# Decay exponents from running sums by head, and the backward weighing on the vector engine

## The chip, the cores and the metric

The kernel runs on one core of a Trainium2 chip. The metric is the device time of one execution in microseconds (us), lower is better. The core has five engines that work side by side, each taking its own instructions in a fixed order: TensorE (PE, matrix products, with its weight loads shown as PEld), VectorE (DVE), ScalarE (ACT), GpSimd (POOL), and SyncE (SP), which here only issues transfers. They wait for each other through semaphores. SBUF is the memory they work in; PSUM holds the results of PE and is read by DVE and ACT.

## What is computed

One layer of an encoder over 256 tokens of 2048 channels, all float32. The part that matters is the bidirectional state-space mixer: with 16 heads, two groups and chunks of 128 tokens, it needs for each head, direction and chunk a 128 x 128 matrix of decays, the exponential of a difference of running sums.

```python
da = jnp.moveaxis((dt * a).reshape(b, c, q, g, e), 2, -1)
acum = jnp.cumsum(da, axis=-1)
...
seg = acum[..., :, None] - acum[..., None, :]
decay = jnp.exp(jnp.where(causal, seg, -jnp.inf))
cb = jnp.einsum("bclgn,bcsgn->bcgls", cmc, bmc)
y_diag = jnp.einsum("bcgls,bcgels,bcsgep->bclgep", cb, decay, xdt)
```

The backward direction does the same on the flipped sequence, and both are added. The state-space mixer stands beside a pooling mixer; both read one input projection (`w_in`) and go through one output projection (`w_out`). A gated convolutional feed-forward network and a gated embedding follow; the change doesn't touch them.

## The kernel before

Every large product is split: a float32 matrix is kept as a rounded high half and a remainder, and three products (high-high, high-low, low-high) replace one. `split` (L139) makes the halves of a weight block: ACT copies the high half (L150), DVE subtracts for the low one (L151). Blocks come through a ring of three raw buffers (`raw`, L154) by transfers on SP's queue, and the halves live in rings of five. `page` (L71) hands out 13 pages of 2048 columns in a ring, `mid` (L74) three of 1024. PSUM has eight banks: six for `main` accumulators, two for `misc`.

The order in time is this. The projection `dtu` (time steps and pooling input) runs first, until about 53 us. Then three slabs of `xbc` follow by `feature_major` (L317): slab 2, slab 0, slab 1, four blocks of weights each, 48 products of 256 columns a block. Behind each slab come `times_rows` (L402), the five-tap convolution `conv` (L410; four ACT instructions `cv` on L416, 16 DVE instructions on L422), a tanh on ACT (L622) and a last product on DVE (L624). Then the projection `z` runs by `token_major` (L285), and `w_out` (`wo`, its products named `woa`) from about 208 us.

Between the blocks the list `work` (L671 to L705) gives small jobs: each block, on ending, takes one entry (`aside`, L194). A scheduler that works on the whole program then decides where each instruction stands on its engine, so that the jobs mostly, not always, stand where the list has them. The jobs that matter:

- `seg_prep(i)` (L552): four POOL products of 512 columns (L558) make, for four heads of one chunk, the time steps `da` (as high half `dah` and remainder `dal`) masked by a triangle, for both directions. `seg(i)` (L562): four PE products with a triangle (`m_gt`, `m_lt`) turn them into the exponents of both directions in one PSUM buffer; ACT takes the exponential into `E` (L567). There are eight of each.
- `decays` (L540): four small PE products `dps` and an exponential give the decays to and from the chunk borders (`dec`).
- `pool_mix`, `pool_map` (L574, L583): the pooling mixer; `pool_map` empties its PSUM buffer by four pairs of ACT and DVE instructions (`cath`, L188, and `catl`, L189).
- `cb` (L596): the products of B and C, masked into `cbm`.
- `weigh(t, g)` (L627): weighs the decays of eight heads: POOL multiplies the backward part (L630), DVE adds the forward part in eight instructions (L635) and multiplies into `E` (L639).
- `xs_turn` (L609): PE transposes of a slab (`xt`), emptied by ACT into `xs` (L614). `far(t)` (L644): POOL makes `xd` from `xs` (L646). `skip(t)`: POOL, L650. `mix(t, g)` (L653): PE product `yo` of `xd`, then DVE, POOL, eight PE products `yd` of `E` and `xs`, and DVE.

`seg`, `decays`, `pool_mix`, `pool_map`, `cb`, `xs_turn` and `mix` all take their PSUM from the two `misc` buffers, in turn.

Of the kernel before, what the change touches and what calls it, by code (L numbers as in the profile page):

```python
# [21 lines left out]
H = 16  # L22
# [29 lines left out]
def build(nc, a, out):  # L52
# [5 lines left out]
    with tile.TileContext(nc) as tc, \  # L58
# [24 lines left out]
        def misc(name):  # L83
            return pc.tile([P, 512], F32, tag="misc", name=name)

        def mm(o, lhsT, rhs, start, stop):
            nc.tensor.matmul(o, lhsT, rhs, start=start, stop=stop, skip_group_check=True)  # L87


        ep = early.enter_context(tc.tile_pool(name="early", bufs=1))  # L90
# [18 lines left out]

        xt = [ep.tile([P, V_SCW + L], F32, name="xt0")] + [page(f"xt{i}") for i in (1, 2)]  # L110
        vt = cp.tile([P, V_N - V_SCW], F32, name="vt")
        small = ep.tile([P, 80 + 512], F32, name="small")

        last, sums_ = {}, {}

        def load(dst, src, ahead=False):

            with tc.issue_after(last["dma"]) if last and not ahead else nullcontext():
                return ins(nc.sync.dma_start(dst, src))
# [8 lines left out]

        last["dma"] = load(xt[0], a["x_cols"][:, :V_SCW + L])
        dtb, alog, dsk = small[:, :32], small[:, 32:64], small[:, 64:80]  # L130
        mask = small[:, 80:].rearrange("p (m f) -> p m f", m=4)

        def vec(i):
            return xt[0][:, i:i + 1] if i < V_SCW else vt[:, i - V_SCW:i - V_SCW + 1]
# [302 lines left out]
        for u in range(0, NK, 2):  # L437
            r = [wp.tile([P, 2048], F32, tag="raw", bufs=3, name=f"dtur{u}") if u else r0, page(f"dtur{u + 1}")]
# [37 lines left out]
        with tc.issue_after(half[0]), tc.issue_after(half[1]):  # L476
            xs_ = [page(f"x{t}") for t in range(2)]
            for t in range(2):
                load(xs_[t], x[t * P:(t + 1) * P, :])
            rx = row_rstd("rx", xs_)  # L480
            m_gt, m_lt = (ep.tile([P, P], F32R, name=n) for n in ("m_gt", "m_lt"))
            nc.vector.tensor_copy(m_gt, mask[:, 2, :])
            nc.vector.tensor_copy(m_lt, mask[:, 3, :])
            aneg = ep.tile([P, 32], F32, name="aneg")
            nc.scalar.activation(aneg, alog, AF.Exp)
            nc.gpsimd.tensor_scalar(aneg, aneg, -1.0, None, op0=ALU.mult)

# [17 lines left out]
        for t in range(2):  # L505
# [3 lines left out]
                                    op0=ALU.mult)  # L509
# [20 lines left out]
        dah = ep.tile([P, 2, 32], F32R, name="dah")  # L530
        dal = ep.tile([P, 2, 32], F32, name="dal")
        nc.vector.tensor_tensor(da, dt, aneg.unsqueeze(1).to_broadcast([P, 2, 32]), op=ALU.mult)
        nc.vector.tensor_copy(dah, da)
        nc.vector.tensor_sub(dal, da, dah.bitcast(F32))

# [14 lines left out]
        steps = {}  # L550

        def seg_prep(i):  # L552
            t, q = divmod(i, 4)
            ap_ = page(f"ap{i}", F32R).rearrange("p (a h l) -> p a h l", a=4, h=4)
            for j in range(4):
                d, src = j // 2, (dah.bitcast(F32), dal)[j % 2]
                hs = slice(d * H + 4 * q, d * H + 4 * q + 4)
                nc.gpsimd.tensor_tensor(ap_[:, j], src[:, t, hs].unsqueeze(2).to_broadcast([P, 4, P]),  # L558
                                        mask[:, d, :].unsqueeze(1).to_broadcast([P, 4, P]), op=ALU.mult)
            steps[i] = ap_  # L560

        def seg(i):  # L562
            t, q = divmod(i, 4)
            sps, ap_ = misc(f"seg{i}"), steps.pop(i)
            for j in range(4):
                mm(sps, (m_gt, m_lt)[j // 2], ap_[:, j].rearrange("p h l -> p (h l)"), j == 0, j == 3)
            nc.scalar.activation(ee[t][:, q * 512:(q + 1) * 512], sps, AF.Exp)  # L567


        cat = Panel.__new__(Panel)  # L570
# [56 lines left out]
        def weigh(t, g):  # L627

            w = mid(f"w{t}{g}")
            nc.gpsimd.tensor_tensor(w.rearrange("p (h l) -> p h l", h=8),  # L630
                                    cbm[:, 1, g, t, :].unsqueeze(1).to_broadcast([P, 8, P]),
                                    dt[:, t, H + 8 * g:H + 8 * g + 8].unsqueeze(2).to_broadcast([P, 8, P]),
                                    op=ALU.mult)
            for h in range(8):
                nc.vector.scalar_tensor_tensor(w[:, h * P:(h + 1) * P], cbm[:, 0, g, t, :],  # L635
                                               dt[:, t, 8 * g + h:8 * g + h + 1], w[:, h * P:(h + 1) * P],
                                               op0=ALU.mult, op1=ALU.add)
            es = ee[t][:, g * 1024:(g + 1) * 1024]
            nc.vector.tensor_mul(es, es, w)  # L639
# [28 lines left out]
        def job(f, *args):  # L668
            return lambda: f(*args)

        xd = {}  # L671
        work.extend([
            [job(seg_prep, 0)],
            [job(seg_prep, 1), job(pool_mix, 0), job(pool_mix, 1)],
            [job(seg_prep, 2), job(pool_mix, 2), job(pool_mix, 3), job(decays)],
            [job(seg_prep, 3), job(seg, 0)],
        ])
        bc = xbc(2)
        work.extend([
            [job(seg_prep, 4), job(seg, 1), job(pool_map, 0), job(pool_map, 1)],  # L680
            [job(seg_prep, 5), job(seg, 2), job(cb, bc, 0), job(cb, bc, 1)],
            [job(seg_prep, 6), job(seg, 3), job(pool_map, 2), job(pool_map, 3)],
            [job(seg_prep, 7), job(seg, 4), job(weigh, 0, 0)],
        ])
        xa = xbc(0)
        work.extend([
            [job(seg, 5), job(weigh, 0, 1)],
            [job(seg, 6), job(xs_turn, xa, 0)],
            [job(seg, 7), job(weigh, 1, 0)],
            [job(weigh, 1, 1)],  # L690
        ])
        xb = xbc(1)
        y = page("y")
# [1 line left out]

        work.extend([
            [],
            [],
            [],
            [job(xs_turn, xb, 1)],  # L700
            [job(far, 1), job(skip, 0), job(far, 0), job(skip, 1)],
            [job(mix, 0, 0)],
# [11 lines left out]
        for t in range(2):  # L714
# [13 lines left out]
            r = rms(f"yn{t}", [ss], rz[t][:, 1:2], n=2)  # L728
# [97 lines left out]
        h = [page(f"h{t}") for t in range(2)]  # L826
# [122 lines left out]
        for half in range(2):  # L949
# [13 lines left out]
            for t in range(2):  # L963
                for n, (o, c0) in enumerate(columns(acc[t])):
                    c1 = c0 + o.shape[-1]
                    c = slice(half * 1024 + c0, half * 1024 + c1)
# [4 lines left out]
                    if end:  # L971
# [3 lines left out]
                                                   op0=ALU.add, op1=ALU.mult)  # L975
                    q = tiny(f"gq{t}{half}{n}", 1)
# [11 lines left out]
def laid_out(a):  # L988

    def cols(*vs):  # L990
        return np.concatenate([v.reshape(-1, P).T for v in vs], axis=1)

    return {
        "x_cols": np.concatenate([cols(a["mix_norm_pre"][0]),
                                  a["x"][0].T.reshape(NK, P, L).transpose(1, 0, 2).reshape(P, NK * L)], axis=1),
        "p_t": a["p"][0, 0].T.reshape(2, P, L).transpose(1, 0, 2),
        "columns": np.concatenate([
            cols(a["ssd_conv_w"][0], a["ssd_conv_b"][0], a["ssd_norm"][0], a["pool_scale"][0], a["ffn_norm_pre"][0],
                 a["ffn_conv_w"][0], a["ple_norm_pre"][0], a["ffn_conv_b"][0]),
            np.broadcast_to(np.concatenate([a[n][0].reshape(-1) for n in ("ssd_dt_bias", "ssd_a_log", "ssd_d")]),  # L1000
                            (P, 80)),
            masks().transpose(1, 0, 2).reshape(P, 4 * P)], axis=1),
    }


def masks():
    j = np.arange(P)[:, None]
    l = np.arange(P)[None, :]
    return np.stack([j <= l, j >= l, j > l, j < l]).astype(np.float32)


def constants():
# [17 lines left out]
```

## Time and profile before

| | |
|---|---|
| time, median of 3 runs | 1143.8 us (1143.8 to 1144.74) |
| the profiled execution | 1143.09 us, its span 1141.3 us |
| mean granted clock of TensorE | 0.997 |
| chain that ended last | PE 90%, DVE 6%, ACT 1%, DMA 1%, issue 1%, POOL 1% |
| `xbc` slab 2, 0, 1 on PE, first product | 52.8 us, 82.2 us, 124.1 us |
| `z` on PE, first product | 151.5 us |
| `woa` on PE, first product | 207.8 us |

The span is the time between the first and the last recorded instruction; the device time has 1.8 us more around it. A busy time of an engine is the sum over its instructions, and matmuls overlap, so that two that start 0.47 us apart are shown with 0.62 us each. What the time follows is the chain that ended last: it is traced back from the last instruction, each time to what released it. The busy shares over the whole span hide the stretch from 80 to 170 us, where DVE is busy for 80 to 100% of each 10 us and POOL for up to 100%.

### The profile page before, as it was taken

What the parts mean: (1) busy time and instruction counts of PE and PEld (TensorE: products, weight loads), DVE (VectorE), ACT (ScalarE), POOL (GpSimd) and SP (SyncE); (2) the same over time, 40 slices, a digit from 0 to 9 for tenths busy, and PEclk for the clock granted to TensorE, in tenths of its full rate; (3) what the DMA queues carried; (4) which work ended last, traced back from release to release, by engine and by line L of the source; (5) the groups of instructions that cost most, each with busy time, mean ns of one, the idle gap of its engine ahead of it and who ended that gap; (6) DMA issues with size and microseconds to landing.
All of it is one profiled execution on the core that took longest, in us unless ns stands there. A gap on an engine that the chain in (4) does not pass through costs nothing.

```text
span 1141.3 us, 15449 instructions
## 1 busy us (share of the span) xinstructions
PE 1122.0 (98%) x6018; PEld 966.0 (85%) x6018; DVE 868.8 (76%) x1140; ACT 611.0 (54%) x830; POOL 124.9 (11%) x124
## 2 busy tenths in 40 slices
PE   9998999999999999999999999999999999999996
PEld 9997987888888888888888888888888888778885
DVE  6579896699876666666766756668888888789895
ACT  6633543565674554444544544545555565656562
POOL 0274504200110000000000000000000000001001
PEclk9999999999999999999999999999999999999999
DMA  9952347555556555555555565556566656666552
GB/s 358 341 184 75 111 151 267 200 160 190 172 190 205 196 190 185 184 185 186 189 191 193 181 204 186 185 184 222 157 212 221 200 170 220 194 221 205 181 196 74
DMA packets 129866, 220.09 MB, mean 193 GB/s; under 512 B 3713, under 2 KB 96769, under 8 KB 128897
## 3 DMA queue, kind: packets, MB, share of 16 engines
q1 hardware_dynamic: 129232, 217.70, 57.4%
q0 software_dynamic: 272, 1.05, 0.5%
q8 instruction: 47, 0.77, 0.3%
q10 hardware_dynamic: 288, 0.36, 0.1%
q14 instruction: 27, 0.21, 0.1%
HBM read 216.99 MB, written 2.10 MB: 192 GB/s over the span
## 4 chain that ended last, share of the span: by engine, by line
PE 90%; DVE 6%; ACT 1%; DMA 1%; issue 1%; POOL 1%; DVEq 0%; POOLq 0%; ACTq 0%
PE va L87 22%; PE ga L87 21%; PE dna L87 15%; PE gt L87 7%; PE woa L87 7%; PE dtu L87 4%; PE z L87 4%; PE xbc L87 3%; DVE cv L422 2%; PE dns L87 1%; PE ple L87 1%; DMA dn134r<-w_ffn_down 1%; PE dn0s L87 1%; DVE w L635 1%; DVE xb_0l L151 1%
## 5 line engine op out<-in xcount | busy, mean ns | idle before, releaser
L87 PE MATMUL ga<-wox,ug_0h 128*128 128x512 f32 x352 | 125.5, 395 | 0.0
L87 PE MATMUL ga<-wox,ug_1h 128*128 128x512 f32 x352 | 125.1, 394 | 0.0
L87 PE MATMUL va<-wox,uv_1h 128*128 128x512 f32 x352 | 124.8, 393 | 0.0
L87 PE MATMUL va<-wox,uv_0h 128*128 128x512 f32 x352 | 124.8, 393 | 0.0
L87 PE MATMUL ga<-wox,ug_1l 128*128 128x256 f32 x352 | 99.1, 282 | 0.0
L87 PE MATMUL ga<-wox,ug_0l 128*128 128x256 f32 x352 | 99.1, 282 | 0.0
L87 PE MATMUL va<-wox,uv_1l 128*128 128x256 f32 x352 | 99.1, 281 | 0.0
L87 PE MATMUL va<-wox,uv_0l 128*128 128x256 f32 x352 | 99.1, 281 | 0.0
L87 PEld LDWEIGHTS va<-wox,uv_0h 128*128 128x128 f32 x352 | 66.1, 188 | 15.0
L87 PEld LDWEIGHTS va<-wox,uv_1h 128*128 128x128 f32 x352 | 66.1, 188 | 15.0
L87 PEld LDWEIGHTS ga<-wox,ug_0h 128*128 128x128 f32 x352 | 66.1, 188 | 14.9
L87 PEld LDWEIGHTS ga<-wox,ug_1h 128*128 128x128 f32 x352 | 66.1, 188 | 14.9
L87 PE MATMUL dna<-dn_0h,hs 128*128 128x512 f32 x248 | 76.2, 395 | 0.8 <-DVE hs L865 0.5
L87 PE MATMUL dna<-dn_1h,hs 128*128 128x512 f32 x248 | 75.7, 393 | 0.0
L848 POOL TENSOR_TENSOR fc<-fc,rfb 128x1024 f32<-128x1024 f32 x11 | 26.6, 2417 | 440.2 <-ACT fc L847 440.2
L87 PEld LDWEIGHTS ga<-wox,ug_0l 128*128 128x128 f32 x352 | 66.2, 188 | 0.1
L87 PEld LDWEIGHTS ga<-wox,ug_1l 128*128 128x128 f32 x352 | 66.2, 188 | 0.0
L87 PEld LDWEIGHTS va<-wox,uv_0l 128*128 128x128 f32 x352 | 66.2, 188 | 0.0
L87 PEld LDWEIGHTS va<-wox,uv_1l 128*128 128x128 f32 x352 | 66.2, 188 | 0.0
L87 PEld LDWEIGHTS dna<-dn_0h,hs 128*128 128x128 f32 x248 | 46.2, 188 | 13.1 <-DVE hs L865 2.5
L87 PEld LDWEIGHTS dna<-dn_1h,hs 128*128 128x128 f32 x248 | 46.5, 188 | 10.8
L87 PE MATMUL dna<-dn_0l,hs 128*128 128x512 f32 x124 | 40.2, 393 | 0.0
(1457 smaller groups left out, 2930.0 us busy)
## 6 DMA issues: line engine op xcount, KB each, us to landing
dn0r<-w_ffn_down SPq DMA_DIRECT2D x16, 1024.0 KB, 5.6
dn1r<-w_ffn_down SPq DMA_DIRECT2D x15, 1024.0 KB, 5.7
zr<-w_in SPq DMA_DIRECT2D x8, 1024.0 KB, 5.1
dtur<-w_in SPq DMA_DIRECT2D x14, 528.0 KB, 8.8
wo0r<-w_out SPq DMA_DIRECT2D x7, 1024.0 KB, 5.9
gt1r<-w_ple_gate SPq DMA_DIRECT2D x7, 1024.0 KB, 6.3
wo1r<-w_out SPq DMA_DIRECT2D x6, 1024.0 KB, 5.7
gt0r<-w_ple_gate SPq DMA_DIRECT2D x6, 1024.0 KB, 5.6
```

The lines of the kernel that those rows point to most:

```text
L87: nc.tensor.matmul(o, lhsT, rhs, start=start, stop=stop, skip_group_check=True)
L151: last["dve"] = ins(nc.vector.tensor_sub(lo[:, s], src[:, s], hi[:, s].bitcast(F32)))
L422: nc.vector.scalar_tensor_tensor(o[:, lo:hi], i[:, lo + d:hi + d], vec(wcol + j * wstep + f), o[:, lo:hi], op0=ALU.mult, op1=ALU.add)
L635: nc.vector.scalar_tensor_tensor(w[:, h * P:(h + 1) * P], cbm[:, 0, g, t, :], dt[:, t, 8 * g + h:8 * g + h + 1], w[:, h * P:(h + 1) * P], ...
L848: nc.gpsimd.tensor_tensor(cv.rearrange("p (f t) -> p f t", f=4), cv.rearrange("p (f t) -> p f t", f=4), rfb.unsqueeze(1).to_broadcast([P, ...
```

## The change

The exponents are no longer made by masking the time steps and multiplying with a triangle. The running sums come first, once for all heads: `da4` (DVE, two instructions) repeats `da` four times, with a minus sign for the backward direction; four float32 products `cps` with the triangles give the running sums of all 16 heads of both chunks and directions in 64 rows, which holds four copies of the 16 heads. ACT makes a rounded high half `seg_h`, DVE the value that each row holds (by the column `low`: in every second group of 16 rows the remainder, in the others the sum itself), and eight ACT copies with row masks (`among`, `four`) place them in two pages: `seg_w`, the weights, and `seg_x`, the columns. Both pages have 128 rows, of which 64 are set to zero by two ACT instructions, and 64 hold heads and patterns, so that one product of 128 rows gives the differences of running sums for four heads.

`seg(i)` is then two products of 512 columns, one for each direction, in two `misc` buffers. ACT copies the first into `E`, DVE takes the smaller of the second and the first (L585 of the changed kernel), and ACT the exponential in place. In the masked half the smaller one is the other direction's exponent.

`weigh` has its product of L630 on `nc.vector` in place of `nc.gpsimd`. The first two weighings stand in slab 1's list, the last two in that of `z`. `seg_prep` is gone, `seg_sums` and the first two `seg` stand in slab 2's list, and the later jobs move in the lists of the slabs. `m_gt`, `m_lt`, `dah` and `dal` are gone. `small` is nine columns wider.

```diff
-            m_gt, m_lt = (ep.tile([P, P], F32R, name=n) for n in ("m_gt", "m_lt"))
-            nc.vector.tensor_copy(m_gt, mask[:, 2, :])
-            nc.vector.tensor_copy(m_lt, mask[:, 3, :])
+            seg_w = page("seg_w", F32R)
+            nc.scalar.activation(seg_w[64:], xs_[0][64:], AF.Copy, scale=0.0)
+            seg_w = seg_w.rearrange("p (a q s) -> p a q s", a=4, q=4)
+            seg_x = page("seg_x", F32R)
+            nc.scalar.activation(seg_x[64:], xs_[0][64:], AF.Copy, scale=0.0)
+            seg_x = seg_x.rearrange("p (a i l) -> p a i l", a=4, i=4)
+            for a_ in range(4):
+                nc.scalar.activation(seg_w[:32, a_], four[:32].unsqueeze(2).to_broadcast([32, 4, P]), AF.Copy,
+                                     scale=-1.0)
+                nc.scalar.copy(seg_x[32:64, a_], among[32:].unsqueeze(2).to_broadcast([32, 4, P]))
...
-        nc.vector.tensor_copy(dah, da)
-        nc.vector.tensor_sub(dal, da, dah.bitcast(F32))
+        for d in range(2):
+            nc.vector.tensor_scalar(da4[:, :, d], da[:, :, d * H:(d + 1) * H].unsqueeze(2).to_broadcast([P, 2, 4, H]),
+                                    1.0 - 2.0 * d, None, op0=ALU.mult)
...
-        def seg_prep(i):
-            t, q = divmod(i, 4)
-            ap_ = page(f"ap{i}", F32R).rearrange("p (a h l) -> p a h l", a=4, h=4)
-            for j in range(4):
-                d, src = j // 2, (dah.bitcast(F32), dal)[j % 2]
-                hs = slice(d * H + 4 * q, d * H + 4 * q + 4)
-                nc.gpsimd.tensor_tensor(ap_[:, j], src[:, t, hs].unsqueeze(2).to_broadcast([P, 4, P]),
-                                        mask[:, d, :].unsqueeze(1).to_broadcast([P, 4, P]), op=ALU.mult)
-            steps[i] = ap_
+        def seg_sums():
+            cps = misc("cps")
+            for a_ in range(4):
+                mm(cps[:64, a_ * P:(a_ + 1) * P], da4[:, a_ // 2, a_ % 2].rearrange("p r h -> p (r h)"),
+                   mask[:, 3 * (a_ % 2), :], True, True)
+            hi, c = page("seg_h", F32R)[:64, :512], page("seg_c")[:64, :512]
+            nc.scalar.copy(hi, cps[:64, :])
+            nc.vector.scalar_tensor_tensor(c, hi.bitcast(F32), low, cps[:64, :], op0=ALU.mult, op1=ALU.add)
+            c4 = c.rearrange("p (a l) -> p a l", a=4)
+            for i in range(4):
+                nc.scalar.activation(seg_x[:32, :, i, :], c4[:32], AF.Copy, scale=among[:32, i:i + 1])
+                nc.scalar.activation(seg_w[32:64, :, i, :], c4[32:], AF.Copy, scale=four[32:, i:i + 1])
 
         def seg(i):
             t, q = divmod(i, 4)
-            sps, ap_ = misc(f"seg{i}"), steps.pop(i)
-            for j in range(4):
-                mm(sps, (m_gt, m_lt)[j // 2], ap_[:, j].rearrange("p h l -> p (h l)"), j == 0, j == 3)
-            nc.scalar.activation(ee[t][:, q * 512:(q + 1) * 512], sps, AF.Exp)
+            ps = [misc(f"seg{i}{d}") for d in range(2)]
+            for d in range(2):
+                mm(ps[d], seg_w[:, 2 * t + d, q], seg_x[:, 2 * t + d].rearrange("p i l -> p (i l)"), True, True)
+            e = ee[t][:, q * 512:(q + 1) * 512]
+            nc.scalar.copy(e, ps[0])
+            nc.vector.tensor_tensor(e, ps[1], e, op=ALU.min)
+            nc.scalar.activation(e, e, AF.Exp)
...
-            nc.gpsimd.tensor_tensor(w.rearrange("p (h l) -> p h l", h=8),
+            nc.vector.tensor_tensor(w.rearrange("p (h l) -> p h l", h=8),
...
-            [job(seg_prep, 0)],
-            [job(seg_prep, 1), job(pool_mix, 0), job(pool_mix, 1)],
-            [job(seg_prep, 2), job(pool_mix, 2), job(pool_mix, 3), job(decays)],
-            [job(seg_prep, 3), job(seg, 0)],
+            [],
+            [job(pool_mix, 0), job(pool_mix, 1)],
+            [job(pool_mix, 2), job(pool_mix, 3), job(decays), job(seg_sums)],
+            [job(seg, 0), job(seg, 1)],
         ])
         bc = xbc(2)
         work.extend([
-            [job(seg_prep, 4), job(seg, 1), job(pool_map, 0), job(pool_map, 1)],
-            [job(seg_prep, 5), job(seg, 2), job(cb, bc, 0), job(cb, bc, 1)],
-            [job(seg_prep, 6), job(seg, 3), job(pool_map, 2), job(pool_map, 3)],
-            [job(seg_prep, 7), job(seg, 4), job(weigh, 0, 0)],
+            [job(seg, 2), job(pool_map, 0), job(pool_map, 1)],
+            [job(cb, bc, 0), job(cb, bc, 1), job(seg, 3)],
+            [job(seg, 4), job(pool_map, 2)],
+            [job(seg, 5), job(pool_map, 3)],
         ])
         xa = xbc(0)
         work.extend([
-            [job(seg, 5), job(weigh, 0, 1)],
-            [job(seg, 6), job(xs_turn, xa, 0)],
-            [job(seg, 7), job(weigh, 1, 0)],
-            [job(weigh, 1, 1)],
+            [job(seg, 6), job(weigh, 0, 0)],
+            [job(seg, 7)],
+            [job(xs_turn, xa, 0), job(weigh, 0, 1)],
+            [],
         ])
...
         work.extend([
             [],
-            [],
-            [],
+            [job(weigh, 1, 0)],
+            [job(weigh, 1, 1)],
             [job(xs_turn, xb, 1)],
```

More of the change, by code (lines that the diff above doesn't have):

```diff
@@ L111, in build @@
         vt = cp.tile([P, V_N - V_SCW], F32, name="vt")
-        small = ep.tile([P, 80 + 512], F32, name="small")
+        small = ep.tile([P, 89 + 512], F32, name="small")
         last, sums_ = {}, {}
@@ L130, in build @@
         dtb, alog, dsk = small[:, :32], small[:, 32:64], small[:, 64:80]
-        mask = small[:, 80:].rearrange("p (m f) -> p m f", m=4)
+        mask = small[:, 80:592].rearrange("p (m f) -> p m f", m=4)
+        low, among, four = small[:64, 592:593], small[:64, 593:597], small[:64, 597:601]
         def vec(i):
@@ L529, in build @@
         da = ep.tile([P, 2, 32], F32, name="da")
-        dah = ep.tile([P, 2, 32], F32R, name="dah")
-        dal = ep.tile([P, 2, 32], F32, name="dal")
+        da4 = ep.tile([P, 2, 2, 4, H], F32, name="da4")
         nc.vector.tensor_tensor(da, dt, aneg.unsqueeze(1).to_broadcast([P, 2, 32]), op=ALU.mult)
-        nc.vector.tensor_copy(dah, da)
-        nc.vector.tensor_sub(dal, da, dah.bitcast(F32))
+        for d in range(2):
+            nc.vector.tensor_scalar(da4[:, :, d], da[:, :, d * H:(d + 1) * H].unsqueeze(2).to_broadcast([P, 2, 4, H]),
+                                    1.0 - 2.0 * d, None, op0=ALU.mult)
         dec = ep.tile([P, 4, H], F32, name="dec")
@@ L549, in build @@
         ee = [page(f"E{t}") for t in range(2)]
-        steps = {}
-        def seg_prep(i):
-            t, q = divmod(i, 4)
-            ap_ = page(f"ap{i}", F32R).rearrange("p (a h l) -> p a h l", a=4, h=4)
-            for j in range(4):
-                d, src = j // 2, (dah.bitcast(F32), dal)[j % 2]
-                hs = slice(d * H + 4 * q, d * H + 4 * q + 4)
-                nc.gpsimd.tensor_tensor(ap_[:, j], src[:, t, hs].unsqueeze(2).to_broadcast([P, 4, P]),
-                                        mask[:, d, :].unsqueeze(1).to_broadcast([P, 4, P]), op=ALU.mult)
-            steps[i] = ap_
+        def seg_sums():
[10 more added lines that the diff above has]
+                nc.scalar.activation(seg_w[32:64, :, i, :], c4[32:], AF.Copy, scale=four[32:, i:i + 1])
         def seg(i):
             t, q = divmod(i, 4)
-            sps, ap_ = misc(f"seg{i}"), steps.pop(i)
-            for j in range(4):
-                mm(sps, (m_gt, m_lt)[j // 2], ap_[:, j].rearrange("p h l -> p (h l)"), j == 0, j == 3)
-            nc.scalar.activation(ee[t][:, q * 512:(q + 1) * 512], sps, AF.Exp)
+            ps = [misc(f"seg{i}{d}") for d in range(2)]
[5 more added lines that the diff above has]
+            nc.scalar.activation(e, e, AF.Exp)
         cat = Panel.__new__(Panel)
@@ L1001, in laid_out @@
                             (P, 80)),
-            masks().transpose(1, 0, 2).reshape(P, 4 * P)], axis=1),
+            masks().transpose(1, 0, 2).reshape(P, 4 * P), head_rows()], axis=1),
     }
@@ L1009, in masks, with head_rows @@
     return np.stack([j <= l, j >= l, j > l, j < l]).astype(np.float32)
+def head_rows():
+    p = np.arange(P)[:, None]
+    i = np.arange(4)[None, :]
+    return np.concatenate([-((p // 16) % 2), p % 4 == i, -1.0 * (p % 16 // 4 == i)], axis=1).astype(np.float32)
 def constants():
```

## The prediction

> **What bounds the kernel now.** I read four views: the busy times of the page, the list of what TensorE waited for, the chain that ended last in the stretch that the change touches (52 to 208 us), and busy time by stretch.
>
> ```profile
> PE 1122.0 (98%) x6018; PEld 966.0 (85%) x6018; DVE 868.8 (76%) x1140; ACT 611.0 (54%) x830; POOL 124.9 (11%) x124
> ```
> ```profile
> PE seg L87 <- DVE catl L189: 4.9, 1, 4.9
> ...
> PE dps L87 <- DVE mixt L581: 0.6, 1, 0.6
> ...
> PE xbc L87 <- DVE xb_0l L151: 0.5, 1, 0.5
> PE yd L87 <- DVE y L666: 0.2, 1, 0.2
> ```
>
> TensorE (PE) is busy 98% of the span, so time is won by taking products off PE or by removing its waits; columns of the last lines are total us, times, longest. All waits of the stretch are here: 6.2 us, of which 4.9 is one wait, for a PSUM buffer that `pool_map` still held. What led to it:
>
> ```profile
> 82.40 1.48 DVE xb_0l L151
> 83.89 13.44 DVE cv L422 x15
> ...
> 98.04 1.14 DVE xb_1l L151
> ...
> 100.23 1.21 DVE cv L624
> ...
> 102.38 0.49 DVE catl L189
> ...
> 103.01 1.80 PE seg L87 x4
> ...
> 125.67 5.59 DVE cv L422 x15
> ```
> ```profile
> 83.80:98.10 14.30, 14.29 (x104) 13.49 (x102) 14.30 (x18) 3.68 (x6) 12.38 (x12) 1.00 0.11 43
> 125.60:132.00 6.40, 6.40 (x52) 6.22 (x51) 6.40 (x18) 3.87 (x6) 0.00 (x0) 1.00 0.33 128
> ```
> ```profile
> 98.00:103.00 5.00, 0.09 (x1) 0.02 (x1) 4.85 (x8) 2.91 (x6) 0.00 (x0) 1.00 0.52 168
> ...
> 104.00:105.00 1.00, 1.00 (x3) 0.75 (x3) 1.00 (x2) 0.77 (x2) 0.00 (x0) 0.50 0.00 0
> ```
>
> The last two fences give, for each stretch, its length, then PE, weight loads, VectorE (DVE), ScalarE (ACT), GpSimd (POOL) busy, then granted clock. The 16 convolution instructions of slab 2 took 14.2 us with POOL busy for 12.4 of them; the same 16 of slab 0 took 6.4 with POOL idle. What POOL does there is `seg_prep` (L558). So its products slow DVE, DVE is 7.8 us late, `pool_map`'s evacuation is late, PE waits 4.9 us. Then PE ran at clock 0.50: the clock was 0.65, 0.50, 0.50, 0.64 in the four microseconds from 103, in all 1.7 us of clock lost.
>
> **Products.** Eight `seg` leave with 32 products of 512 columns; two start 0.47 us apart (81.23, 81.70), so 0.233 each: -7.4. Sixteen of the same shape come: +3.7. `cps` adds four float32 products of 128 columns: two such (`rxbp`) took 0.36, so 0.7; four `dps` of 16 columns took 0.91. I take 0.9. All on PE: **-2.8**.
>
> **Waits that go.** `seg_prep`'s 32 POOL instructions (1.0 to 2.0 us each) vanish, and slab 2's convolution should take 6.4 instead of 14.2. It starts later: eight new ACT copies of 512 elements (`seg_x`, `seg_w`; 0.53 each back to back by the 0.62 row of `pth`) and a `seg` copy (0.60) stand before the slab's `cv` on ACT, so DVE starts it about 2 us later, and three `min` (0.6 each, below) come between; it still ends near 94 instead of 98. The split behind it, L624 and `catl` follow at once. I take the 4.9 as gone, with the **1.7** of half clock. The 0.6 before `dps` comes from a slowed split (1.90 at 73.03 against 1.22 elsewhere); 0.2 should stay: **-0.4**. The 0.5 at 146 came behind L635 at 0.48 each under POOL's L630 (0.27 in the first group): **-0.5**.
>
> **What DVE gets.** Four weighing products of 1024 elements, SBUF to SBUF: 1.21 by the row of L639, together 4.8. Eight `min` of 512 reading PSUM: 0.69 (L666), 0.6 back to back, 5. One `seg_c` 0.7, two `da4` 0.2 each; two casts and the `dah`, `dal` pair (0.2 each) leave. Net +10.5. It no longer suffers POOL: 7.8 in the convolution, some 2 in the splits at 65 to 82 (1.5 to 1.9 instead of 1.2), 3.4 in L635 (16 at 0.48 instead of 0.27). The balance is about -3. But it moves: in the built program the second weighing pair stands between the splits of `z`, and PE comes there earlier, so the split of the fourth `z` row block is due about when it is done. Bounds 0 and 1.5; nearest is the 0.5 at 146, also a split behind weighing: **+0.5**.
>
> **What ACT gets.** Ahead of the `xb2` split: two copies of 64x2048 (1.92 by the row of `rxj`) and eight of 32x512: 8 us. ACT was free there from 41.1 on but for three instructions, so the first `xb2` high half ends near 50.6 and its low half at 51.8; PE wants them at 52.8. Cost 0, cover 0.9 us; if the copies take 1 us more it becomes a wait of that size. The transfers of `pt`, `pmat` and `poolw` now stand behind one more `xb2r` on SP's queue; their first readers (64 us for `mx`) are 20 us off.
>
> **A new wait.** The jobs of slab 1 and `z` are in another order. In the built program's PE order the eight `xt` transposes of slab 1 are now followed directly by the product `yo` of `mix(0, 0)`; before, 48 `z` products (11 us) lay between. `yo` needs `xd`, a POOL product that needs `xs`:
>
> ```profile
> 173.78 1.03 PE L613 MATMUL xt<-ident,cv 128*128 128x128 f32 x8
> 175.35 1.08 ACT L614 ACTIVATE xs<-xt 128x512 f32<-128x512 f32 x2
> 176.51 1.96 POOL L646 TENSOR_TENSOR xd<-xs,dec 128x1024 f32<-128x1024 f32 x1 [33.20 <-ACT xs L614]
> ```
>
> PE is free 0.8 us after `xt` starts; the first `xs` can start about then, the two take 1.1, then 0.1, `xd` 1.96, 0.1: PE idle 3.0. The second `xd` here took 2.88 beside a busy DVE, and DVE will be busy: up to 3.9. I take **+3.2**, nearer the first. Everything on PE queues behind `yo`.
>
> The Trainium skill speaks against this edit: "TensorE: Matmul & The Clock Gate" (the table "Why this matters for your kernels") wants no PE idle gap over about 3 us, else the clock halves; its Part 1 puts the window at 3.4 us, free-running. The trace agrees as far as it goes, with the 4.9 us gap that was followed by half clock and the 0.6 us gap that was not. By the table the new gap costs the half-clock stretch as well (rival A); by the window it mostly doesn't.
>
> **PSUM pairs.** `misc` has two buffers and each `seg` now takes both: one is free after the ACT copy (0.60), the other after copy and `min`, about 1.5 us after the products. Between a `seg` and the next taker stand 6 to 17 `xbc` products of 0.12 (0.7 to 2 us) in the built order, so most is covered. Tightest is `pool_map(1)`: it takes the buffer of the third pair, whose `min` stands behind all 16 convolution instructions (93.5 against 93.7). Bounds 0 and 8 x 1.5 = 12; nearest are the short waits of 0.2 to 0.6 above, at four places: **+1.0**.
>
> **Sum.** -2.8 - 4.9 - 1.7 - 0.4 - 0.5 + 3.2 + 0.5 + 1.0 = **-5.6**. Behind 208 us PE is the chain nearly alone and nothing is edited, so it should reach the end. The profiled execution took 1143.1 (span 1141.3 and 1.8 around it), 0.7 under the median of 1143.8: 1137.5 in its terms, **1138.2** against the median.
>
> **Rivals.**
> A. The gap before `yo` halves the clock once more: +1.7, 1139.9. For: 4.9 did. Against: it is shorter by 1 to 2 us. Chance 0.26.
> B. The PSUM pairs block PE at every `seg`: 12 instead of 1.0, 1149. For: `min` queues on a DVE that was 80 to 100% busy from 80 to 170 us. Against: the `xbc` between. It decides once the waits pass 0.8 us per pair, where the gain is gone. Chance 0.10.
> C. The slow convolution is not POOL's doing. Then the third `min` comes near 101, `pool_map(1)` waits 7.6 instead of the 4.9, and the new DVE work (some 7.5 from slab 0 on) lands before `z`: -2.8 - 0.4 + 2.7 + 3.2 + 7.5 = +10, 1154. Decides from about 0.65 us an instruction. Against: the two windows above. Chance 0.05.
> D. The gain is given back: PE comes earlier to weights whose transfers don't. For: ACT waited 3.6 and 3.3 us for `zr`. Against: no PE wait ended on a transfer there. 1143.8, chance 0.07.
>
> **Chances and range.** The forecast has 0.52, its own range 1136.3 to 1140.0: below, -7.5 with `yo` at 3.0 and nothing for `dps`, `z` and the pairs; above, `yo` at 3.9, `z` at 1.5 and 0.2 more for the pairs. Under 0.2% (2.3 us) a measurement of this kernel cannot be told from no change. Faster: forecast and A, 0.78; the same: D and a little of B, 0.08; slower: B and C, 0.14. The range takes in A and D, and below half a us for the spread of the runs (0.9 among three): 1135.8 to 1143.8.
>
> **What would show it.** Slab 2's convolution at 0.40 an instruction (C: 0.65 or more); no 4.9 us wait on `catl`; a PE wait `yo` on POOL `xd` of 3.0 to 3.9; the clock in the 4 us behind it 1.00 (A: 0.5); `seg` and `pw` waits of about 1 in all (B: over 6); a start of `woa` near 202 instead of 207.8. The forecast is wrong if PE starts `xbc` after 53.5, or if `z` waits for its splits by more than 1.5.

## The result, and the profile after

| | before | after |
|---|---|---|
| median of the runs taken side by side, 20 each | 1144.07 us (1143.63 to 1145.74) | 1145.89 us (1144.54 to 1147.23) |
| profiled execution (span) | 1143.09 us (1141.3) | 1145.88 us (1144.1) |
| mean granted clock | 0.997 | 0.993 |
| first `z` product on PE | 151.5 us | 142.4 us |
| first `woa` product on PE | 207.8 us | 210.3 us |
| from the one to the other | 56.3 us | 67.9 us |

The ratio is 1.0014, its 95% interval 1.0008 to 1.0020. By the ratio the time went up by 1.6 us where 1138.2 us was forecast, and it lies outside the range (1135.8 to 1143.8). The table already says where. Up to `z` the changed kernel gained 9.1 us; between `z` and `woa` it lost 11.6. Behind `woa` the two spans part by no more than another 0.3 us. (The spans part by 2.8 us, more than the medians, because the profiled execution before was 1.0 us under its median.)

The busy times of the page after (busy us, share of the span, number of instructions):

```profile
PE 1122.4 (98%) x6010; PEld 966.6 (84%) x6010; DVE 865.9 (76%) x1151; ACT 629.8 (55%) x857; POOL 76.3 (7%) x88
```

DVE has 2.9 us less to do than before (868.8), which is the balance of -3 that the prediction had worked out, and POOL has 49 us less. What TensorE waited for in the same kernel (total, times, longest, us):

```profile
PE yo L87 <- POOL xd L665: 7.9, 1, 7.9
...
PE seg L87 <- ACT seg_x L575: 0.7, 1, 0.7
...
PE z L87 <- DVE z_1l L153: 0.4, 1, 0.4
```

The 4.9 us on `catl`, the 0.6 before `dps` and the 0.5 before `xbc` are gone, as forecast. The wait of `yo` for `xd` is there too, but it is 7.9 us and not 3.0 to 3.9. The view of single lines gives durations in ns (lowest, median, highest) and the first and last start; here are the slab 2 convolution before and after, and after the short products of the weighing over the whole run:

```profile
L422 DVE SCALAR_TENSOR_TENSOR cv<-xr,vt,cv x16: 470/1254/1258, 83.8 to 97.6; 128x254 f32<-128x254 f32 x8, 128x255 f32<-128x255 f32 x8
```
```profile
L424 DVE SCALAR_TENSOR_TENSOR cv<-xr,vt,cv x16: 475/482/485, 87.0 to 93.6; 128x254 f32<-128x254 f32 x8, 128x255 f32<-128x255 f32 x8
```
```profile
L654 DVE SCALAR_TENSOR_TENSOR w<-cbm,dt,w x32: 337/347/2002, 129.6 to 170.6; 128x128 f32<-128x128 f32 x32
```

With POOL idle, all 16 of the convolution have 0.48 us each, where their median was 1.25 before. So the first link of the prediction's chain is shown. The highest of L654, 2.00 us where most have 0.35, belongs to the stretch that went wrong. Here it is as a timeline (start, length of the row, engine, line, what; in brackets the idle time before it and what ended it), first PE, then POOL, then DVE:

```profile
155.18 1.03 PE L632 MATMUL xt<-ident,cv 128*128 128x128 f32 x8
164.08 1.22 PE L87 MATMUL yo<-xd,cbm 128*128 128x512 f32 x1 [7.87 <-POOL xd L665]
```
```profile
157.03 7.00 POOL L665 TENSOR_TENSOR xd<-xs,dec 128x1024 f32<-128x1024 f32 x1 [80.39 <-issue]
163.99 1.94 POOL L669 TENSOR_TENSOR y<-xs,small 128x1024 f32<-128x1024 f32 x1
165.90 1.95 POOL L665 TENSOR_TENSOR xd<-xs,dec 128x1024 f32<-128x1024 f32 x1
167.81 1.95 POOL L669 TENSOR_TENSOR y<-xs,small 128x1024 f32<-128x1024 f32 x1
```
```profile
154.40 2.19 DVE L654 SCALAR_TENSOR_TENSOR w<-cbm,dt,w 128x128 f32<-128x128 f32 x8
156.50 1.23 DVE L153 TENSOR_TENSOR z_0l<-zr,z_0h 128x1024 fp32r<-128x1024 f32 x1
...
161.04 1.23 DVE L153 TENSOR_TENSOR z_0l<-zr,z_0h 128x1024 fp32r<-128x1024 f32 x1
162.18 8.78 DVE L654 SCALAR_TENSOR_TENSOR w<-cbm,dt,w 128x128 f32<-128x128 f32 x8
170.88 1.21 DVE L153 TENSOR_TENSOR z_1l<-zr,z_1h 128x1024 fp32r<-128x1024 f32 x1
```

Read the DVE rows against the POOL rows. From 156.5 to 162.2 DVE runs five instructions of 1.23 us (three splits, L658 and L649) with no gap, none of them slowed, and the one POOL product beside them takes 7.00 us instead of 1.96: POOL is kept out. From 162.2 on POOL gets through, at its clean 1.95 for each of the next three products, and now DVE pays: eight short products take 8.78 us, where the same eight took 2.19 at 154.4. PE stands still through the first half of this.

The same place in the view by stretches (length; busy time of PE, weight loads, DVE, ACT, POOL; granted clock; DMA):

```profile
156.00:164.00 8.00, 0.22 (x2) 0.00 (x0) 8.00 (x9) 1.95 (x3) 6.97 (x2) 0.74 0.44 143
164.00:170.00 6.00, 5.92 (x12) 4.06 (x13) 6.00 (x5) 0.35 (x1) 5.75 (x4) 0.50 0.07 30
```

DVE is busy without a break. The clock is 0.50 from 159.8 to 170.1 us; PE works from 164.1 on, so 6.0 us of work were at half clock, a loss of 3.0. Together 7.9 + 3.0 + 0.4 (the wait for `z_1l`) = 11.3 of the 11.6 us.

### The profile page after: what moved, and what is told of

Same layout as the page of the kernel before. It is cut to its first block, busy times and chain, and to the rows that moved or that the text cites. A ratio compares the mean times of both kernels' runs of the same rounds, so it can differ in the third digit from the quotient of the medians.

```text
span 1144.1 us, 15428 instructions
## 1 busy us (share of the span) xinstructions
PE 1122.4 (98%) x6010; PEld 966.6 (84%) x6010; DVE 865.9 (76%) x1151; ACT 629.8 (55%) x857; POOL 76.3 (7%) x88
## 4 chain that ended last, share of the span: by engine, by line
PE 87%; issue 8%; DVE 2%; POOL 1%; ACT 1%; DMA 1%; DVEq 0%; POOLq 0%; ACTq 0%
PE va L87 21%; PE ga L87 21%; PE dna L87 15%; PE gt L87 7%; PE woa L87 7%; PE dtu L87 4%; PE z L87 3%; PE xbc L87 2%; PE dns L87 1%; PE ple L87 1%; DMA dn134r<-w_ffn_down 1%; PE dn0s L87 1%; POOL xd L665 1%; PE dn1s L87 0%; PE yd L87 0%
```

## The experiments

The wait that the trace names is `yo` on `xd`. Whether it is the cause is another question, since DVE is busy all through it and might have kept `z` waiting anyway. A table of all kernels but the two that only time instructions stands at the end of this section.

**e1: the wait of `yo` alone taken away.** `mix(0, 0)` is queued on PE behind its own place, so that 92 `z` products stand between `xt` and `yo`.

```diff
-            nc.tensor.matmul(o, lhsT, rhs, start=start, stop=stop, skip_group_check=True)
+            last["pe"] = ins(nc.tensor.matmul(o, lhsT, rhs, start=start, stop=stop, skip_group_check=True))
...
+        def held(f, *args):
+            def run():
+                with tc.issue_after(last["pe"]):
+                    f(*args)
+            return run
...
-            [job(mix, 0, 0)],
+            [held(mix, 0, 0)],
```

> The changed kernel with one edit: the product `yo` of `mix(0, 0)` is queued on PE behind the `z` products of its own place (92 `z` products between `xt` and `yo` instead of none). Theory S (the changed kernel loses its gain at one place: `yo` waits 7.9 us for POOL's `xd`, and the clock is halved for 6 us of work behind it, 3.0 us): no wait of `yo` on `xd`, clock 1.00 through `z`, `xd` itself still slow (over 3 us), `woa` starts about 10.9 us earlier than in the changed kernel, time 1134 to 1137. Rival R (DVE is the bound from slab 1 on, and the wait at `yo` only gave it time to catch up): `z` now waits for its low halves by 6 us or more in all, time 1142 or more.

1145.25 us, ratio 1.0009 (1.0000 to 1.0018): no better than after by more than 0.6 us. Waits of TensorE in that kernel:

```profile
PE z L87 <- DVE z_1l L153: 6.5, 2, 6.0
PE z L87 <- DVE z_0l L153: 1.6, 1, 1.6
```

The 7.9 us on `xd` became 8.1 us on the splits of `z`, and the clock was at 0.50 for 6.8 us behind them. The wait that the trace had named was a cover. The theory that `yo` is the cause falls; its rival, that DVE is the bound, holds.

**e2 and e3: the two halves of the change apart.** e2 is the changed kernel with the product of `weigh` back on GpSimd. (The edit moves more than the product: in its trace `xt` stands behind 96 `z` products and not 52, and `yo` 48 behind it, so `far` and `skip` no longer run beside the weighing.)

```diff
-            nc.vector.tensor_tensor(w.rearrange("p (h l) -> p h l", h=8),
+            nc.gpsimd.tensor_tensor(w.rearrange("p (h l) -> p h l", h=8),
```

> The new exponents alone: the changed kernel with the weighing product back on GpSimd, at the changed places of the jobs. In this program `yo` stands 48 `z` products behind `xt` again. Theory S: no wait of `yo`; the gain of the first part stays (first `z` product near 142.4 to 144 instead of 151.5), time 1135 to 1139, a little above e1 because four POOL products slow DVE's L654. Rival R2 (the weighing on DVE is what brought the gain, the exponents none): time 1142 or more, and the wait of 4.9 us on `catl` is back.

e3 is the kernel before with the weighing on VectorE, spread over slab 1 and `z` as in the change, and the exponents as they were:

```diff
-            nc.gpsimd.tensor_tensor(w.rearrange("p (h l) -> p h l", h=8),
+            nc.vector.tensor_tensor(w.rearrange("p (h l) -> p h l", h=8),
...
-            [job(seg_prep, 7), job(seg, 4), job(weigh, 0, 0)],
+            [job(seg_prep, 7), job(seg, 4)],
...
-            [job(seg, 5), job(weigh, 0, 1)],
-            [job(seg, 6), job(xs_turn, xa, 0)],
-            [job(seg, 7), job(weigh, 1, 0)],
-            [job(weigh, 1, 1)],
+            [job(seg, 5), job(weigh, 0, 0)],
+            [job(seg, 6)],
+            [job(seg, 7), job(xs_turn, xa, 0), job(weigh, 0, 1)],
+            [],
...
-            [],
-            [],
+            [job(weigh, 1, 0)],
+            [job(weigh, 1, 1)],
```

> The weighing alone: the kernel before with its four weighing products on DVE, the first two in slab 1's list, the last two in that of `z`; exponents as before. 68 `z` products stand between `xt` and `yo`. Theory S: the wait of 4.9 us on `catl` and the half clock behind it stay, since `seg_prep` still runs beside slab 2's convolution (16 instructions in 13 to 15 us); no wait of `yo`; time 1142 to 1145. Rival R2: the wait on `catl` is gone and the time is under 1140.

e2: 1142.76 us, ratio 0.9990 (0.9981 to 0.9999). e3: 1147.07 us, 1.0026 (1.0017 to 1.0035). So the exponents without the move of the weighing are worth 1 us, the move alone costs 3, and neither time shows the 9 us that the changed kernel had gained up to `z`. Both times miss theory S, e2 by 3.8 us above its 1139 and e3 by 2.1 above its 1145. R2 falls: the wait on `catl` is gone in e2. In e3 the 4.9 us on `catl` stay, and a `z` wait of 1.8 us comes with the weighing between the splits. In e2 the gain up to `z` is there (its `z` starts at 142.9), and the loss behind it has another form, in its DVE rows:

```profile
159.86 4.07 DVE L654 SCALAR_TENSOR_TENSOR w<-cbm,dt,w 128x128 f32<-128x128 f32 x9 [1.79 <-POOL w L649]
...
166.83 1.21 DVE L153 TENSOR_TENSOR z_1l<-zr,z_1h 128x1024 fp32r<-128x1024 f32 x1
```

DVE waits 1.79 us for a POOL product, which had itself taken 4.99 us beside DVE's row, then runs slowed beside the next, and the split behind it comes 5.2 us late for PE. In both kernels the weighing of chunk 1 stands ahead of splits of `z` on DVE.

**e4 and e8: the two engines side by side, alone.** Four POOL products of the form of L665 per stage, beside a row of one kind of DVE instruction:

```diff
+            for k in range(4):
+                nc.gpsimd.tensor_tensor(by(o), by(sync), far, op=ALU.mult)
+            for k in range(n):
+                f(d, k)
...
+        stage("scaled", 40, lambda d, k: nc.vector.scalar_tensor_tensor(
+            d[:, k % 8 * 128:(k % 8 + 1) * 128], one[:, :128], sm[:, k % 8:k % 8 + 1],
+            two[:, k % 8 * 128:(k % 8 + 1) * 128], op0=ALU.mult, op1=ALU.add))
...
+        stage("bank", 30, lambda d, k: nc.vector.tensor_tensor(d[:, :512], bank, two[:, :512], op=ALU.mult))
```

> No part of the encoder is computed (x is copied to the output). Five stages one after the other, each four POOL products of 128x1024 of the form of `xd` beside a stream of DVE instructions: none; two-input subtractions of 1024; the form of L635 with 128; single-input products of 1024; products of a PSUM operand with 512. Theory S: alone 1.9 to 2.0 us each; beside the two-input subtractions of 1024 a POOL product lasts over 4 us, or until the stream ends, with DVE hardly slowed (1.14 to 1.25 a piece); beside the short L635 form POOL keeps about 2 us and DVE is slowed from 0.26 to over 0.45. Rival W (`xd` was slow because POOL had idled for 80 us before it): only the very first POOL product is slow, the four beside the subtractions take 2 to 3 us each.

Groups of e4 (busy us, mean ns of one; the DVE means hold also the instructions that ran on when POOL was done):

```profile
L89 DVE TENSOR_TENSOR dtwo<-x,x 128x1024 f32<-128x1024 f32 x20 | 30.8, 1541 | 0.7
...
L94 DVE TENSOR_TENSOR dbank<-bank,x 128x512 f32<-128x512 f32 x30 | 20.7, 691 | 1.0
L90 DVE SCALAR_TENSOR_TENSOR dscaled<-x,sm,x 128x128 f32<-128x128 f32 x40 | 17.3, 507 | 0.0
L80 POOL TENSOR_TENSOR otwo<-stwo,sm 128x1024 f32<-128x1024 f32 x4 | 10.7, 2672 | 0.3
...
L80 POOL TENSOR_TENSOR oalone<-salone,sm 128x1024 f32<-128x1024 f32 x4 | 8.1, 2028 | 0.3
```

With both inputs in SBUF, DVE and POOL slow each other: a short instruction of 0.26 us takes about 2.0, one to each POOL product, and a long one of 1.22 about 2.8. A DVE instruction with an input in PSUM isn't slowed (0.69 with POOL and without). The Trainium skill, "SBUF — State Buffer" (section "Who interferes with whom"), says as much: a DVE instruction with two SBUF inputs contends with a GpSimd instruction that reads SBUF, over a pair of ports that only one of them holds at a time. The long product of e4 with a single input, in SBUF, was slowed too (2.27 us instead of 0.69). Four POOL products, four turns of some 2.0 us and four short ones: that is the 8.78 us of L654 in the changed kernel. What e4 doesn't show is a POOL product of over 4 us, which theory S expected of it, or of 7. In it each DVE instruction waited for the one before, through the destination that they share. e8 gives eight of them a destination each:

```diff
+        ring = [sb.tile([P, 1024], F32, name=f"r{k}") for k in range(8)]
+        stage("two", 8, lambda d, k: nc.vector.tensor_sub(ring[k], one, two))
```

> The port by itself, nothing of the encoder computed: GpSimd products 128x1024 as in line 665 beside two-input VectorE subtractions into eight different destinations with no wait between them (stage two), and into one destination again (stage again). If VectorE's unbroken row keeps GpSimd out, the GpSimd product takes 5 us or more and VectorE's instructions stay near 1.22 us each; if they take turns as in e4, GpSimd takes 2 to 3 us and VectorE's instruction about 2 us or more in both stages.

Nothing held the eight back, so they ran beside the products of the first stage:

```profile
7.36 10.92 POOL L80 TENSOR_TENSOR oalone<-salone,sm 128x1024 f32<-128x1024 f32 x4
8.32 15.58 DVE L90 TENSOR_TENSOR r<-x,x 128x1024 f32<-128x1024 f32 x8 [0.32 <-DMA x<-x]
```

They took turns again: 2.67 us for a POOL product, up to 2.92 for DVE's. So a DVE row without waits is not enough to keep POOL out for 7.00 us. But POOL had started first here (7.36 against 8.32 us), while in the changed kernel DVE was in its row when POOL came (156.50 against 157.03). e8 doesn't try that order, and what decides whose turn it is stays open (the last section comes back to it).

**e5: `far` and `skip` away from the weighing.** The theory from here on, T2: DVE is the bound from slab 1 to the fourth `z` block, because the change brings PE there 9 us earlier, and 6.6 us (8.78 - 2.19) of DVE's lateness are its turns with `far` and `skip`. Those start with `xt`, which stands 52 `z` products into `z`. e5 queues `xt` behind its own place.

```diff
-            [job(xs_turn, xb, 1)],
+            [held(xs_turn, xb, 1)],
```

> The kernel after with xt of slab 1 queued on TensorE behind its own place (96 z products, xt, 48 z products, yo) instead of behind 52 of them, so that far (xd) and skip start some 9 us later on GpSimd. Theory T2 (VectorE is the bound from slab 1 to z, and loses about 6.6 us because far and skip run beside the short products of line 654: 8.78 us for a group that takes 2.19 us elsewhere): line 654 of chunk 1 takes 2 to 3 us, the TensorE waits of z for its splits fall from the 8.1 us of the run with yo held back to about 1.5, no 0.5 clock after 145 us, time 1134 to 1138. Rival T2' (VectorE is the bound by its added work alone, minimums and weighing, and the contention only eats time that it would idle): line 654 gets short but the z waits stay at 6 us or more, with one or two half-clock windows behind them, time 1142 to 1146.

1140.02 us, ratio 0.9962 (0.9949 to 0.9974). Its DVE rows and its waits:

```profile
162.12 2.20 DVE L654 SCALAR_TENSOR_TENSOR w<-cbm,dt,w 128x128 f32<-128x128 f32 x8
164.22 1.23 DVE L153 TENSOR_TENSOR z_1l<-zr,z_1h 128x1024 fp32r<-128x1024 f32 x1
```
```profile
PE z L87 <- DVE z_0l L153: 2.5, 1, 2.5
...
PE z L87 <- DVE z_1l L153: 0.5, 1, 0.5
```

The group starts at the same time as in the changed kernel and takes 2.20 instead of 8.78. Against e1, where `z` doesn't wait for `xd` either, the waits fall from 8.1 to 3.0 and the time by 5 us. The contention is shown as the larger part, and T2' falls with it. T2's own numbers weren't met in full: the time is 2 us above its bound, and a wait of 2.5 us with 3.4 us of half clock is left.

**e6 and e7: the weighing between the splits.** e6 is e5 without the two weighings of chunk 1:

```diff
-            [job(weigh, 1, 0)],
-            [job(weigh, 1, 1)],
+            [],
+            [],
```

> The kernel of e5 with both weighings of chunk 1 (line 649, two groups of about 9.3 us together between slab 1 and z) left out: the decays of chunk 1 are not weighed, the output differs. T2 and T2' both expect the z waits gone (under 1 us) and no 0.5 clock behind 145 us: time 1132 to 1135. If z still waits over 2 us, VectorE's load is not what holds z.

e7 keeps them, behind the mixing of chunk 0, and queued on DVE behind the splits of that unit. (It has e5's hold of `xt` too.)

```diff
+        def behind(f, *args):
+            def run():
+                with tc.issue_after(last["dve"]):
+                    f(*args)
+            return run
...
-            [job(weigh, 1, 0)],
-            [job(weigh, 1, 1)],
+            [],
+            [],
...
-            [job(mix, 0, 0)],
-            [job(mix, 0, 1), job(mix, 1, 0)],
+            [job(mix, 0, 0), behind(weigh, 1, 0)],
+            [job(mix, 0, 1), job(mix, 1, 0), behind(weigh, 1, 1)],
```

> The kernel of e5 with the two weighings of chunk 1 moved behind the mixing of chunk 0 in z (queued on VectorE behind the splits of that z unit), so that z's first splits don't queue behind them; nothing is left out. T2 and T2': z waits under 1.5 us, no 0.5 clock behind 145 us, time 1133 to 1137. If the later weighing holds up yd or a later z split by over 3 us, the loss returns there: 1141 to 1146.

e6: 1135.71 us, ratio 0.9922 (0.9908 to 0.9936), 0.7 above the expected range with its waits as expected. e7: 1135.70 us, 0.9924 (0.9912 to 0.9937). The weighing of chunk 1 costs nothing that can be measured where it now stands. The `z` wait of e7, and one of its DVE rows:

```profile
PE z L87 <- DVE z_1l L153: 0.4, 1, 0.4
```
```profile
162.13 1.23 DVE L153 TENSOR_TENSOR z_0l<-zr,z_0h 128x1024 fp32r<-128x1024 f32 x1 [0.91 <-ACT z_0h L152]
```

DVE now idles between the splits until the high halves come, instead of being late with its own. The clock stays at 1.00 through `z`. This kernel beats both: by the ratios it is 8.7 us under the one before and 10.3 under the changed one.

**e9 and e10: each of the two causes once more.** e9 is e5 with the weighing's product back on GpSimd (the edit of e2). In the traces the instructions of e9 and e2 stand in the same order on every engine, since `xt` stood at that place in e2 already: e9 is e2 once more, with e5 as its partner.

> The kernel of e5 (xt of slab 1 held behind its own place) with the first product of the weighing (line 649, four of 1.23 us) back on GpSimd: the change without its move to VectorE, in a mended order. If VectorE's added work is what is left of the loss in e5 (z waits 3.0 us and one half-clock window), the z waits fall under 1.5 us and the time to 1136 to 1138. If the GpSimd products take turns with VectorE's short ones of line 654 as they did in the run with the weighing on GpSimd (line 654 at 4.07 us for a group), VectorE wins nothing: z waits 2 us or more, 1139 to 1143.

1143.39 us, 0.9990 (0.9981 to 0.9999), the ratio of e2; it is the second branch, 0.4 us above its range: L654 at 4.07 us behind a wait of 1.79 for POOL, as in e2, and a `z` wait of 5.5. Against it the move of the weighing to VectorE (e5) wins 3.2 us.

e10 is e7, without its hold, with `xt`, `far` and `skip` one unit earlier in the list of `z`: POOL's products then run beside DVE's splits, with no weighing between them.

```diff
             [],
             [],
-            [],
             [job(xs_turn, xb, 1)],
             [job(far, 1), job(skip, 0), job(far, 0), job(skip, 1)],
+            [],
```

> The kernel of e7 (weighings of chunk 1 behind the mixing in z) with xt of slab 1, far and skip one z unit earlier (24 z products earlier on TensorE): far and skip then run on GpSimd beside VectorE's splits of z while VectorE still catches up. If far and skip beside the splits cost VectorE what they cost it beside line 654 in the kernel after, z waits 3 us or more and the time is 1139 to 1143; if VectorE has room for it once the weighing is out of the way, z waits stay under 1 us and the time is 1135 to 1137.

1135.75 us, 0.9928 (0.9915 to 0.9942), as good as e7, with the same `z` wait of 0.4. Its DVE rows show the contention all the same:

```profile
163.00 2.15 DVE L153 TENSOR_TENSOR z_0l<-zr,z_0h 128x1024 fp32r<-128x1024 f32 x1 [1.55 <-ACT z_0h L152]
...
170.78 2.90 DVE L153 TENSOR_TENSOR z_1l<-zr,z_1h 128x1024 fp32r<-128x1024 f32 x1
```

Four splits at 2.2 to 2.9 us instead of 1.2 cost nothing here, since DVE had idled just before them. Contention costs time where the slowed engine is already the late one.

All in one view. "Waits" are PE's for the splits of `z` and for `xd`; "half clock" is the time at 0.50 between 145 and 210 us; times in us.

| kernel | weighing of chunk 1 | beside `far`, `skip` | waits | half clock | `z` to `woa` | median | ratio |
|---|---|---|---|---|---|---|---|
| before | ahead of `z`, product on POOL | no | 0 | 0 | 56.3 | 1144.1 | |
| after | between splits, DVE | yes | 8.3 | 10.2 | 67.9 | 1145.9 | 1.0014 |
| e1 | between splits, DVE | yes | 8.1 | 6.8 | 67.5 | 1145.3 | 1.0009 |
| e2 | between splits, product on POOL | no | 5.2 | 3.4 | 63.2 | 1142.8 | 0.9990 |
| e3 | between splits, DVE | no | 1.8 | 3.4 | 59.8 | 1147.1 | 1.0026 |
| e5 | between splits, DVE | no | 3.0 | 3.4 | 61.3 | 1140.0 | 0.9962 |
| e6 | left out | no | 0.4 | 0 | 56.9 | 1135.7 | 0.9922 |
| e7 | behind the mixing, DVE | no | 0.4 | 0 | 55.1 | 1135.7 | 0.9924 |
| e9 | between splits, product on POOL | no | 5.5 | 3.4 | 63.4 | 1143.4 | 0.9990 |
| e10 | behind the mixing, DVE | no | 0.4 | 0 | 55.0 | 1135.8 | 0.9928 |

(In e7 and e10 `woa` starts before the last `yd`, so their `z` to `woa` is a little short.) Of the 10.3 us between the changed kernel and e7, 5.9 go by the ratios to `far` and `skip` beside the weighing (after against e5; 5.4 against e1, where `yo` doesn't wait either) and 4.3 to the weighing ahead of the splits (e5 against e7), each with its share of half clock.

## Why the prediction was wrong

**Up to `z` its steps mostly held.** Products -2.8, the `catl` wait -4.9, the half clock behind it -1.7, `dps` -0.4, `xb_0l` -0.5 and the PSUM pairs +1.0 make -9.3; the first `z` product came 9.1 us earlier. That POOL made the convolution slow is shown: rival C falls. No PE wait was on a `misc` buffer: rival B falls. The one new wait in the stretch was 0.7 us on `seg_x`, which had no term: ACT's eight copies behind `seg_sums` took 0.72 us each where 0.53 was taken. PE started `xbc` at 52.7 us, against 52.8 before. That the two sums agree to 0.2 us is partly luck: the waits and the half clock that went make 7.7, the +1.0 for the pairs didn't come, the 0.7 did, and 2.1 are left for the products.

**The step that failed** is "What DVE gets", in its last sentences: the weighing pair "stands between the splits of `z`, and PE comes there earlier, so the split of the fourth `z` row block is due about when it is done", with the bounds 0 and 1.5 and **+0.5**. The balance over DVE, "about -3", was right (-2.9), though its own terms of +10.5 add up to 10.1, and though it holds the 6.6 us of L654's contention, which it didn't foresee. The error is that it was treated as one account. What was saved lay in front, at 84 to 98 us, and PE took it and came to `z` 9.1 us earlier. What was added lies between 150 and 171 us, where DVE then had no slack: with `yo` out of the way, the splits of `z` were 8.1 us late and not 0.5. Two things were missing from the term. One is the contention. `far` and `skip` were seen to move, but only the price that DVE sets on POOL's `xd` was asked for, not theirs on DVE's L654, though the same paragraph credits 3.4 us for the end of just such contention on L635. (In the kernel before, `far` and `skip` had slowed three splits from 178.7 us on to 2.7 to 2.8 us each, where PE waited for none of them.) That was 5.9 us with its half clock. The other is the plain queue of 9 us of weighing ahead of the splits, 4.3 us with its half clock. The sign that the prediction had set for this step, a `z` wait of over 1.5, stayed at 0.4 in the changed kernel, since DVE caught up while PE stood at `yo`.

**The `yo` term**, +3.2 with bounds of 3.0 and 3.9, had the right place and the wrong size: 7.9, since `xd` took 7.00 us and not 1.96 to 2.88. Its upper bound came from a row where the two engines alternated; here five DVE instructions went first. The size decides little, as the wait lies beside DVE's lateness and not behind it: without it the time is the same within 0.6 us.

**Rival A**, half clock behind the gap, did happen, with a loss of 3.0 us instead of 1.7, as a part of this larger loss. The rule by which the Trainium skill, "TensorE: Matmul & The Clock Gate" (table "Why this matters for your kernels"), spoke against the edit, no PE gap over about 3 us, was borne out by the 7.9 us gap; but shorter gaps were enough here too, 2.46 us in e5 and 1.80 in e3. **Rival D** falls: no PE wait in `z` ended on a transfer, and e7 turns 8.7 of the 9.1 us into time.

**The rival that was missing** is that the gain in front makes DVE the bound behind. The profile before had its sign: DVE was busy for 32.3 of the 34 us from 142 to 176 us already, as its view by stretches has it (length; busy time of DVE; granted clock; DMA):

```profile
142.00:176.00 34.00, 32.29 (x50) 1.00 0.54 183
```

(The upper end of the forecast's own range, 1140.0, adds up to 1140.1 by its terms.)

## What to carry to other kernels

When an edit brings the bounding engine earlier to a place, sum the next engine's work there stretch by stretch, and not over the span: a saving in front pays for no work behind. Work that nobody needs yet, like this weighing, belongs behind the splits that the bounding engine is about to want; put there, it cost nothing that could be measured. Where GpSimd and VectorE both read SBUF, price the contention for both sides, and before going after the wait that a trace names, look whether another engine was late through all of it.

## What the hardware showed that was not expected

- Whose turn it is between DVE and POOL stays open. In the changed kernel one POOL product took 7.00 us (clean 1.95) while DVE lost nothing, then DVE's short ones took up to 2.00 us while POOL lost nothing. Four more products were kept out like this: 7.01 us in e1, 4.99 in e2 and in e9, and 9.56 in e3, where PE had other work:

```profile
170.94 9.56 POOL L646 TENSOR_TENSOR xd<-xs,dec 128x1024 f32<-128x1024 f32 x1 [45.90 <-ACT xs L614]
```

All five began while DVE was inside a row of 1.2 us instructions without a gap, and ended 1.8 us behind the last of that row. Where POOL had come first (e5, e8, e10), the two took turns and both paid, up to 2.9 us each. But a product of e2 at 126.4 us began inside such a row too and took 2.75, so the order of the starts alone doesn't decide it. POOL's idling of 80 us ahead of the 7.00 is not the reason: in e5 `xd` took 1.90 after 95 us.

- Half clock came behind waits of under 3 us: 2.46 us in e5 and 1.80 us in e3 were each followed by 3.4 us at 0.50, and 1.58 us in e1 was not. All the stretches at 0.50 in the table are 3.41 us long, or two or three times that, and start a whole number of 3.41 us behind the start of full clock (in the changed kernel 159.83 against 6.23 us, 45 times; in e1 171.34 against 7.50, 48 times). On that grid, worked out from the traces, the 2.46 lies in one period (154.91 to 158.33), the 1.80 too (169.93 to 173.34), and the 1.58 is cut by an edge at 157.68. So a gap's cost also hangs on where it falls: the 4.9 us on `catl` were followed by 3.4 us at 0.50 in the kernel before and by 6.8 in e3. After the 7.9 us gap full clock came back 6.0 us after PE had resumed, at the end of the first period that PE had worked through.
